# A third load buffer, a cast held in program order and a separate gate buffer in a two-model kernel

## The chip, the cores and the metric

The kernel runs on one core of a Trainium2 chip. The metric is the device time of one execution in microseconds. Three runs of the kernel before gave 2311.27 us (median), 2310.58 and 2315.97 us.

## The reference

The input is 512 tokens of width 1024, all in float32. Two hybrid layers come first, then one block of another kind. Cut to what matters here, a hybrid layer is:

```
h   = rmsnorm(x, pre_mix_g);  proj = h @ w_in          # 12 kinds of columns, gates among them
y_a = deltanet(proj) @ w_up_dn                         # its output is normed and gated by silu(z)
y_b = sliding_window_attention(proj) @ w_up_sw
mix = (sigmoid(gate_a) * y_a + sigmoid(gate_b) * y_b) @ w_o
x   = x + rmsnorm(mix, post_mix_g)
ff  = square(relu(rmsnorm(x, pre_mlp_g) @ w_ff1)) @ w_ff2   # 1024 -> 4096 -> 1024
x   = x + rmsnorm(ff, post_mlp_g)
```

The second block (a state-space branch, a pooling branch, gates, an output product and a last norm) is not touched by the change.

## The kernel before

Activations stand transposed: 8 tiles of 128 features by 512 tokens. Each float32 operand is kept as a high part `h` (a cast to float32r) and a low part `lo` (source minus `h`), and each product is three matmuls: `h·h`, `h·lo`, `lo·h`, in that order (`mm3`). A weight block is 1024x128. `load_w` (L225) fetches it by a DMA on the SyncE queue (SP) into a `raw` tile, of which there are two, casts it on ScalarE (ACT) to `h` (L241) and forms `lo` on VectorE (L242). The result goes to `wh`/`wl` rings of three, or, for weights that are kept for a second use, into tiles `kw` that a callback `keep` allocates. After `third(pool)` (L164), and once two more loads have gone by, every load whose running number leaves 2 when divided by 3 goes to an extra buffer `rawx` in that pool. In the kernel before this is on in the mixing stage, the last down stage and the second block.

Stages of a layer, as far as the change goes:

- **Mixing** (L1304). `fetch` (L1313) loads a tile from DRAM into a ring `fe` of three buffers. For each of 8 output blocks it fetches the deltanet output (`ogf`) and gate 0, multiplies them on VectorE (L1335), splits the product into `ah`, and after the attention branch's matmuls multiplies by gate 2 (L1340), which also stands in the `fe` ring. Then come 8 blocks with `w_up_dn` on `ah`, then 8 with `w_o`, the last in two halves of 256 tokens.
- **First six blocks of the MLP** (L1403 on). Six `w_ff1` blocks are run over the first half of the tokens, then again over the second, so the last three are kept. The residual and norm of the mixing stage's second half (`residual`, a generator that `tick` moves on after blocks 0 and 1) run beside them; its results are stored to DRAM (`xd_mid`) through a ring of four tiles `rt`.
- **Last down stage** (L1464 to L1508). The hidden tiles of the last quarter come from four pairs of blocks (`fast_pair`), the last of which feeds hidden tiles 6 and 7. `halves3` runs the first three `w_ff2` blocks over the first half of the tokens with tiles 7 and 6 last. Blocks 3 to 7 load their weight in the loop and keep it. After each block VectorE adds the result into `acc` (L1490) and `fs.add` squares it on ACT (L365). The second half runs the same eight blocks with the weights kept. `tick` there moves on the residual of the first half: its sums follow block 0, its broadcast block 1, the next norm's sums block 5, its broadcast block 6.

The order on each engine is not the order of the program: a planner simulates the kernel and, on each engine, issues what is ready, earlier traced instructions first. `tc.keep_in_program_order(i)` takes this freedom from one instruction: it is issued behind the instruction that was traced just before it on the same engine. `tick` uses it for TensorE: the first matmul after a tick is held behind what the tick issued, and what the tick issues first is held behind the block ahead of it.

Of the kernel before, what the change touches and what calls it, by code (L numbers as in the profile page):

```python
# [19 lines left out]
P = 128  # L20
# [3 lines left out]
KD = D // P  # L24
# [30 lines left out]
def body(  # L55
# [10 lines left out]
    V, S, G, DMA = nc.vector, nc.scalar, nc.gpsimd, nc.sync  # L66
# [89 lines left out]
    def t2(name, shape=(P, SEQ), dtype=F32):  # L156
        return tp.tile(list(shape), dtype, tag="t2", name=name, bufs=NT2)
# [6 lines left out]
    def third(pool):  # L164
        turn[1:] = pool, turn[0] + SKIP
# [56 lines left out]
            V.tensor_tensor(out=lo, in0=t, in1=f32(h), op=ALU.subtract)  # L222
            return h, lo

    def load_w(src, kn=KD, n=P, pool_h=False, keep=None):  # L225
        turn[0] += 1
        if turn[0] % 3 == 2 and turn[1] is not None and turn[0] > turn[2]:
            raw = turn[1].tile([P, kn, n], F32, tag="rawx", name="rawx", bufs=1)
        else:
            raw = wp.tile([P, kn, n], F32, tag="raw", name="raw", bufs=2)  # L230
        DMA.dma_start(out=raw, in_=src.rearrange("(k p) n -> p k n", p=P))
        h = lo = None
        if keep is not None:
            h, lo = keep(kn, n), keep(kn, n)
        if h is None:
            h = wp.tile([P, kn, n], F32R, tag="wh", name="wh", bufs=3)
            lo = wp.tile([P, kn, n], F32R, tag="wl", name="wl", bufs=3)
        if pool_h:
            G.tensor_scalar(out=h, in0=raw, scalar1=1.0, scalar2=0.0, op0=ALU.mult, op1=ALU.add)  # L239
        else:  # L240
            S.copy(out=h, in_=raw)  # L241
        V.tensor_tensor(out=lo, in0=raw, in1=f32(h), op=ALU.subtract)  # L242
        return h, lo

# [197 lines left out]
    def ticks(gen, at):  # L442
        cnt = [0]

        def tick():
            if cnt[0] in at:
                T.turn = True
                next(gen, None)
                T.turn = True
            cnt[0] += 1  # L450
        return tick
# [740 lines left out]
    def layer(l, st, nxt):  # L1192
# [4 lines left out]
        dg = [dp.tile([P, KD, SEQ], F32, name=f"dg{l}{i}") for i in range(3)]  # L1197
# [41 lines left out]
        for _ in range(5):  # L1239
            t = qa.tile([P, 2, 4, 256], F32R, tag="q8", name="kq", bufs=5)  # L1240
# [63 lines left out]
        with sbuf(f"mx{l}") as mp:  # L1304
            third(mp)
            def m2(name, dtype=F32R):
                t = mp.tile([P, 2, SEQ], dtype, tag="m2", name=name, bufs=NM2)
                return t[:, 0, :], t[:, 1, :]

            def keep(kn, n):  # L1310
                return mp.tile([P, kn, n], F32R, tag="m2", name="kw", bufs=NM2)

            def fetch(src, n, name):  # L1313
                t = mp.tile([P, SEQ], F32, tag="fe", name=name, bufs=3)
                DMA.dma_start(out=t, in_=src[:, n, :])
                return t

            def gate(i, n):
                t = fetch(dg[i], n, "gate")
                if (i, n) in plain:  # L1320
                    S.activation(out=t, in_=t, func=gate_fn[i])
                return t

            bo, ao = [], []
            for n in range(KD):
                hl = m2("bh")
                split(*hl, fetch(db, n, "bf"), eng=G)
                bo.append(hl)
            tb = []
            for n in range(KD):  # L1330
                if n % 2 == 0:
                    pair = m2("tb", F32)
                w = load_w(w_up_sw[l][:, n * P:(n + 1) * P])
                t = fetch(og, n, "ogf")
                V.scalar_tensor_tensor(out=t, in0=t, scalar=pcol("dn_norm", l), in1=gate(0, n), op0=ALU.mult, op1=ALU.mult)  # L1335
                hl = m2("ah")
                split(*hl, t)
                ao.append(hl)
                ps = dense(w, bo)
                V.tensor_tensor(out=pair[n % 2], in0=ps, in1=gate(2, n), op=ALU.mult)  # L1340
                tb.append(pair[n % 2])
            mix = []
            for n in range(KD):
                ps = dense(load_w(w_up_dn[l][:, n * P:(n + 1) * P]), ao)
                ta_ = gate(1, n)
                V.tensor_tensor(out=ta_, in0=ps, in1=ta_, op=ALU.mult)
                V.tensor_tensor(out=ta_, in0=ta_, in1=tb[n], op=ALU.add)
                hl = m2("mh")
                split(*hl, ta_)
                mix.append(hl)  # L1350
            mo = [mt.tile([P, SEQ], F32, tag="mo", name="mo", bufs=KD) for _ in range(KD)]
            mid = Stream("pre_mlp", l * KD, f"xd_mid{l}", mt, False)
            wk, tick = {}, None
            for i in range(2):
                ms = Stats(mt)
                for n in range(KD):
                    if i == 0:
                        wk[n] = load_w(w_o[l][:, n * P:(n + 1) * P], keep=keep if n >= 3 else None)
                    ps = dense_half(wk[n], mix, i)
                    V.tensor_copy(out=mo[n][:, HALVES[i]], in_=ps)  # L1360
                    ms.add(mo[n][:, HALVES[i]])
                    if i:
                        tick()
                pending = residual(st, mo, ms.rstd, "post_mix", l * KD, mid, i)
                if i == 0:
                    before = pending
                    tick = ticks(before, AT_O)
            finish(before)

        with sbuf(f"ff{l}") as ff, ExitStack() as es2:  # L1370
# [14 lines left out]
            def up(n, m=1):  # L1385
                return w_ff1[l][:, n * P:(n + m) * P], m == 2

            def down(g, n):
                return w_ff2[l][g * D:(g + 1) * D, n * P:(n + 1) * P], False
# [8 lines left out]
            with sbuf(f"kf{l}") as kp:  # L1398
                def keep(kn, n):
                    return kp.tile([P, kn, n], F32R, tag="kw", name="kw", bufs=2 * (NFF - 3))  # L1400

                tick = ticks(pending, AT_FF)
                wk = [load_w(up(n)[0], keep=keep if n >= 3 else None) for n in range(NFF)]  # L1403
                for i in range(2):
                    for n in range(NFF):
                        if i == 0:
                            hid.append(hidden())
                        relu2(dense_half(wk[n], mid.xs, i), hid[n][0][:, HALVES[i]], hid[n][1][:, HALVES[i]])
                        tick()
                        if i and n < 3:  # L1410
                            w.free("ring")
                    finish(pending)
                    w.fetch(1)
                tail.close()
            tail = ExitStack()
            tl = tail.enter_context(sbuf(f"tl{l}", "right"))
# [46 lines left out]
            kp = es2.enter_context(sbuf(f"kp{l}"))  # L1463
# [15 lines left out]
            wk = {}  # L1479
            for i in range(2):  # L1480
                fs = Stats(tr)
                for n in range(KD):
                    if i == 0 and n == 0:
                        wk = {j: w.take() for j in range(3)}
                        head = halves3([wk[j] for j in range(3)], i)
                    elif i == 0 and n >= 3:
                        wk[n] = load_w(down(3, n)[0], keep=keep)
                    ps = head[n] if i == 0 and n < 3 else dense_half(wk[n], hid, i)
                    ac = acc[n][:, HALVES[i]]
                    V.tensor_tensor(out=ac, in0=ps, in1=ac, op=ALU.add)  # L1490
                    fs.add(ac)
                    if i:
                        tick()

                def ff_rstd(i=i, fs=fs):
                    fm = small((P, 2), "fm")
                    V.scalar_tensor_tensor(out=fm, in0=fs.sums(), scalar=1.0 / D, in1=rs4[i], op0=ALU.mult, op1=ALU.mult)
                    V.tensor_scalar(out=fm, in0=fm, scalar1=EPS, scalar2=None, op0=ALU.add)
                    fr = power(fm, 2)
                    V.tensor_tensor(out=fr, in0=fr, in1=rs2[i], op=ALU.mult)  # L1500
                    return fr

                pending = residual(mid, acc, ff_rstd, "post_mlp", l * KD, xst, i)
                if i == 0:
                    before = pending
                    tick = ticks(before, AT_D)
# [17 lines left out]
    dg = dp.tile([P, 32, SEQ], F32, name="dg2")  # L1524
# [16 lines left out]
    with sbuf("kp2") as kp:  # L1541
        def keep(kn, n):
            return kp.tile([P, kn, n], F32R, tag="kw", name="kw", bufs=2 * NB2 - 6)
# [15 lines left out]
    with sbuf("ss") as sp:  # L1559
# [59 lines left out]
        for g8 in range(4):  # L1619
# [14 lines left out]
            for par in range(2):  # L1634
                V.tensor_copy(out=yv[:, par, 4 * g8:4 * g8 + 4],
                              in_=ps[64 * par:64 * par + 64].rearrange("p q (j c) -> p q j c", c=16))
# [52 lines left out]
    for c in range(4):  # L1689
        ps = dense(load_w(ssm_w_glu_2[0][:, c * P:(c + 1) * P], 4), glu)  # L1690
        t = t2("glt")
# [23 lines left out]
    wk = {}  # L1715
# [53 lines left out]
```

## Time and profile before

| what | value |
|---|---|
| profiled execution, its own time | 2315.69 us |
| its span, first to last instruction | 2313.9 us |
| mean granted TensorE clock | 0.982 |
| TensorE matmul busy / weight loads busy | 2243.0 us (97%) / 1954.5 us (84%) |
| VectorE, ScalarE, GpSimd busy | 1485.3, 952.1, 609.4 us |
| moved by DMA | 284.33 MB, mean 123 GB/s |

The span is the time from the first to the last instruction of the profiled execution; 1.8 us of its own time lie around it. Busy times of different engines overlap. A granted clock of 1 is 2.4 GHz, 0.5 is 1.2 GHz.

### The profile page before, as it was taken

To read this page: it belongs to the slowest core of one execution; us is meant where nothing else is said; L and a number is where in the kernel's file an instruction comes from. 1 tells how busy PE (TensorE), PEld (TensorE's weight loads), DVE (VectorE), ACT (ScalarE), POOL (GpSimd) and SP (SyncE) were. 2 spreads that over 40 slices of the span, in tenths; PEclk is the share of its full clock that TensorE was granted. 3 is DMA by queue.
4 is the path that set the end of the run, shared out by engine and by line. 5 is a ranking of instruction groups with operands and counts; after the bars stand their busy time and mean duration, and the time that the engine had idled before them with its cause. 6 is when DMAs were issued, how large, how long until landed. Compare 5 with 4: busy or idle time off the path is not lost. (4 is left out here: it accounts for less than half of the span.)

```text
span 2313.9 us, 37654 instructions
## 1 busy us (share of the span) xinstructions
PE 2243.0 (97%) x14460; PEld 1954.5 (84%) x14460; DVE 1485.3 (64%) x2958; ACT 952.1 (41%) x1726; POOL 609.4 (26%) x675
## 2 busy tenths in 40 slices
PE   8999999999999999999999999999999999899998
PEld 7867888887989899988678888889898898877788
DVE  5579793445576777665797934465777775435645
ACT  4554333333464354444533333334643444423333
POOL 1643420200336123246333202003351242200001
PEclk9999999999999999999999999999999999999999
DMA  5223424565453433342233345654434334563344
GB/s 177 62 72 87 101 83 128 172 200 160 121 157 92 128 107 98 116 125 58 77 87 88 92 127 182 201 164 126 136 101 118 114 97 123 169 165 117 108 131 146
DMA packets 466431, 284.33 MB, mean 123 GB/s; under 512 B 48502, under 2 KB 440012, under 8 KB 465740
## 3 DMA queue, kind: packets, MB, share of 16 engines
q1 hardware_dynamic: 462544, 280.69, 41.9%
q8 instruction: 114, 1.87, 0.3%
q10 hardware_dynamic: 3708, 1.24, 0.3%
q14 instruction: 65, 0.53, 0.1%
HBM read 235.76 MB, written 46.11 MB: 122 GB/s over the span
## 5 line engine op out<-in xcount | busy, mean ns | idle before, releaser
L78 PE MATMUL psm<-xsh,wh 128*128 128x512 f32 (+1 forms) x1136 | 445.6, 393 | 2.6 <-ACT wh L241 1.6
L78 PE MATMUL psm<-xsl,wh 128*128 128x512 f32 (+1 forms) x1136 | 432.6, 381 | 8.2 <-DVE xsl L342 4.2
L78 PE MATMUL psm<-xsh,wl 128*128 128x512 f32 (+1 forms) x1136 | 431.6, 380 | 0.0
L242 DVE TENSOR_TENSOR wl<-raw,wh 128x1024 fp32r<-128x1024 f32 (+2 forms) x179 | 213.3, 1192 | 89.9 <-ACT wh L241 63.6
L78 PEld LDWEIGHTS psm<-xsh,wh 128*128 128x128 f32 x1136 | 217.6, 192 | 48.4 <-issue 8.6
L78 PEld LDWEIGHTS psm<-xsl,wh 128*128 128x128 f32 x1136 | 218.1, 192 | 45.9 <-DVE xsl L342 5.5
L78 PEld LDWEIGHTS psm<-xsh,wl 128*128 128x128 f32 x1136 | 217.3, 191 | 40.9
L241 ACT CAST wh<-raw 128x1024 fp32r<-128x1024 f32 (+3 forms) x126 | 123.4, 980 | 253.6 <-PE psm L78 218.2
L370 POOL TENSOR_TENSOR sa<-sa,sq 128x256 f32<-128x256 f32 x54 | 51.5, 955 | 665.8 <-ACT sq L365 381.5
L78 PE MATMUL psm<-hh,wh 128*128 128x512 f32 (+1 forms) x480 | 177.1, 375 | 6.4 <-ACT hh L336 6.4
L78 PE MATMUL psm<-hl,wh 128*128 128x512 f32 (+1 forms) x480 | 177.7, 372 | 0.8 <-DVE hl L339 0.8
L78 PE MATMUL psm<-hh,wl 128*128 128x512 f32 (+1 forms) x480 | 176.7, 370 | 0.0
L221 ACT CAST wh<-raw 128x1024 fp32r<-128x1024 f32 x67 | 70.2, 1050 | 127.4 <-PE psm L78 76.2
L221 ACT CAST wh<-raws 128x1024 fp32r<-128x1024 f32 x63 | 66.0, 1047 | 127.9 <-PE psm L78 93.7
L222 DVE TENSOR_TENSOR wl<-raw,wh 128x1024 fp32r<-128x1024 f32 x67 | 97.4, 1454 | 26.0 <-ACT wh L221 23.5
L78 PEld LDWEIGHTS psm<-hh,wh 128*128 128x128 f32 x480 | 90.5, 191 | 22.8 <-ACT hh L336 7.0
L78 PEld LDWEIGHTS psm<-hl,wh 128*128 128x128 f32 x480 | 91.5, 191 | 16.4 <-DVE hl L339 1.3
L78 PEld LDWEIGHTS psm<-hh,wl 128*128 128x128 f32 x480 | 91.6, 191 | 15.1
L222 DVE TENSOR_TENSOR wl<-raws,wh 128x1024 fp32r<-128x1024 f32 x63 | 93.6, 1486 | 13.2 <-ACT wh L221 13.2
L239 POOL TENSOR_SCALAR wh<-raw 128x1024 fp32r<-128x1024 f32 (+1 forms) x53 | 62.9, 1186 | 121.0 <-PE psm L78 104.0
L78 PE MATMUL psm<-ah,wh 128*128 128x512 f32 x256 | 83.0, 405 | 5.2 <-ACT ah L336 5.0
L78 PE MATMUL psa<-xsh,wh 128*128 128x256 f32 x288 | 82.3, 286 | 0.0
(670 smaller groups left out, 5662.5 us busy)
## 6 DMA issues: line engine op xcount, KB each, us to landing
raw<-in_w_in_dram SPq DMA_DIRECT2D x130, 512.0 KB, 3.9
raw<-in_w_ff_dram SPq DMA_DIRECT2D x75, 512.0 KB, 4.1
raws<-in_w_ff_dram SPq DMA_DIRECT2D x51, 512.0 KB, 4.3
gate<-dg SPq DMA_DIRECT2D x48, 256.0 KB, 4.4
rawx<-in_w_in_dram SPq DMA_DIRECT2D x14, 512.0 KB, 4.1
raw<-in_w_up_sw_dram SPq DMA_DIRECT2D x12, 512.0 KB, 5.0
raw<-in_w_up_dn_dram SPq DMA_DIRECT2D x11, 512.0 KB, 4.5
raw<-in_w_o_dram SPq DMA_DIRECT2D x10, 512.0 KB, 4.7
```

What stands on the lines that cost most here:

```text
L78: return s.issue(nc.tensor.matmul(*a, **k))
L221: S.copy(out=h, in_=t)
L222: V.tensor_tensor(out=lo, in0=t, in1=f32(h), op=ALU.subtract)
L239: G.tensor_scalar(out=h, in0=raw, scalar1=1.0, scalar2=0.0, op0=ALU.mult, op1=ALU.add)
L241: S.copy(out=h, in_=raw)
L242: V.tensor_tensor(out=lo, in0=raw, in1=f32(h), op=ALU.subtract)
L370: (G if s.n in POOL_ACC else V).tensor_tensor(out=s.acc, in0=s.acc, in1=sq, op=ALU.add)
```

## The change

`load_w` gets a parameter `pin`, which holds the ACT cast in program order; the loads of blocks 3 to 7 in the last down stage set it. `third(kp)` turns the third raw buffer on for the first six blocks of the MLP and `third(None)` turns it off behind them. Gate 2 of the mixing stage is fetched into a tile of the ring `t2` (four buffers of the same size, used there by nothing else in this stage).

```
-    def load_w(src, kn=KD, n=P, pool_h=False, keep=None):
+    def load_w(src, kn=KD, n=P, pool_h=False, keep=None, pin=False):
...
-            S.copy(out=h, in_=raw)
+            i = S.copy(out=h, in_=raw)
+            if pin:
+                tc.keep_in_program_order(i)
         V.tensor_tensor(out=lo, in0=raw, in1=f32(h), op=ALU.subtract)
...
             def gate(i, n):
-                t = fetch(dg[i], n, "gate")
+                if i == 2:
+                    t = t2("gate2")
+                    DMA.dma_start(out=t, in_=dg[i][:, n, :])
+                else:
+                    t = fetch(dg[i], n, "gate")
...
                 tick = ticks(pending, AT_FF)
+                third(kp)
                 wk = [load_w(up(n)[0], keep=keep if n >= 3 else None) for n in range(NFF)]
...
                     w.fetch(1)
+                third(None)
                 tail.close()
...
                     elif i == 0 and n >= 3:
-                        wk[n] = load_w(down(3, n)[0], keep=keep)
+                        wk[n] = load_w(down(3, n)[0], keep=keep, pin=True)
```

## Rows read from the trace of the kernel before

**Rows 1.** The page, busy time of each engine (share of the span, instructions).
```profile
PE 2243.0 (97%) x14460; PEld 1954.5 (84%) x14460; DVE 1485.3 (64%) x2958; ACT 952.1 (41%) x1726; POOL 609.4 (26%) x675
```
**Rows 2.** Waits of TensorE: us in total, times, longest us.
```profile
PE psm L78 <- ACT hh L336: 6.4, 2, 4.4
...
PE psm L78 <- ACT ft L1380: 5.4, 2, 2.7
PE psm L78 <- ACT ah L336: 5.0, 2, 2.8
```
**Rows 3.** Timeline of ACT, second layer's last pair and after: start, us, instruction.
```profile
1919.52 1.04 ACT L241 CAST kw<-raw 128x1024 fp32r<-128x1024 f32 x1 [1.64 <-DMA raw<-in_w_ff_dram]
...
1930.63 0.42 ACT L365 ACTIVATE sq<-acc 128x256 f32<-128x256 f32 x1 [1.05 <-DVE acc L1490]
```
**Rows 4.** Timeline of TensorE in the same stretch.
```profile
1923.79 1.01 PE L78 MATMUL psm<-hh,wh 128*128 128x256 f32 x3 [4.42 <-ACT hh L336]
```
**Rows 5.** Timeline of ACT, first layer's last pair.
```profile
943.95 1.04 ACT L241 CAST kw<-raw 128x1024 fp32r<-128x1024 f32 x1 [1.26 <-DMA raw<-in_w_ff_dram]
```
**Rows 6.** Stretches: us, each engine's busy us (instructions), granted clock, DMA share, GB/s.
```profile
530.00:536.00 6.00, 6.00 (x16) 4.70 (x16) 4.82 (x6) 1.85 (x3) 0.00 (x0) 0.52 0.70 220
943.00:953.00 10.00, 7.22 (x36) 6.72 (x37) 4.77 (x8) 4.32 (x7) 0.73 (x1) 0.66 0.56 162
1508.00:1511.00 3.00, 2.78 (x8) 2.23 (x8) 2.31 (x4) 1.45 (x2) 0.00 (x0) 0.58 0.89 285
1919.00:1929.00 10.00, 5.00 (x23) 4.30 (x22) 5.42 (x7) 6.97 (x10) 0.00 (x0) 0.66 0.61 174
1929.00:1944.00 15.00, 15.00 (x126) 15.00 (x127) 5.42 (x12) 2.67 (x7) 1.94 (x2) 1.00 0.13 36
```
**Rows 7.** Timeline of VectorE, mixing stage of the first layer.
```profile
514.53 0.75 DVE L1335 SCALAR_TENSOR_TENSOR ogf<-ogf,prm,gate 128x512 f32<-128x512 f32 x1 [4.09 <-DMA gate<-dg]
...
516.93 0.69 DVE L1340 TENSOR_TENSOR tb<-psm,gate 128x512 f32<-128x512 f32 x1
...
522.03 0.75 DVE L1335 SCALAR_TENSOR_TENSOR ogf<-ogf,prm,gate 128x512 f32<-128x512 f32 x1 [3.28 <-DMA gate<-dg]
```
**Rows 8.** Timeline of the SP queue there.
```profile
517.05 1.12 SPq L1315 DMA_DIRECT2D gate<-dg  x2
```
**Rows 9.** Timeline of the SP queue, first six blocks of the second layer's MLP.
```profile
1598.53 0.39 SPq L231 DMA_DIRECT2D raw<-in_w_ff_dram  x1
1598.97 5.09 SPq L1072 DMA_DIRECT2D lbr<-in_ssm_b_re_dram  x1
...
1612.79 0.41 SPq L401 DMA_DIRECT2D xd_mid<-rt  x1
```
**Rows 10.** Timeline of ACT there.
```profile
1610.18 1.04 ACT L241 CAST kw<-raw 128x1024 fp32r<-128x1024 f32 x1 [10.37 <-DMA raw<-in_w_ff_dram]
```
**Rows 11.** Timeline of VectorE there.
```profile
1611.25 1.23 DVE L242 TENSOR_TENSOR kw<-raw,kw 128x1024 fp32r<-128x1024 f32 x1 [7.58 <-ACT kw L241]
```
**Rows 12.** Timelines of VectorE, then ACT, behind one block of the last down stage.
```profile
1934.91 0.42 DVE L1490 TENSOR_TENSOR acc<-psm,acc 128x256 f32<-128x256 f32 x1 [1.48 <-PE psm L78]
...
1935.43 0.42 ACT L365 ACTIVATE sq<-acc 128x256 f32<-128x256 f32 x1 [2.46 <-DVE acc L1490]
```
**Rows 13.** Instructions of tile kw: count, then ns min/median/max, first and last start.
```profile
L241 ACT CAST kw<-raw x24: 1030/1044/1055, 573.5 to 1993.4; 128x1024 fp32r<-128x1024 f32 x24
L242 DVE TENSOR_TENSOR kw<-raw,kw x24: 1215/1225/1762, 574.6 to 1994.5; 128x1024 fp32r<-128x1024 f32 x24
```
**Rows 14.** Timeline of TensorE, second half of the same stage: sums and broadcasts of the residual.
```profile
1946.23 0.50 PE L78 MATMUL psa<-ones,sa 128*128 128x1 f32 x4
...
1965.03 0.60 PE L78 MATMUL psa<-ident,rstd 128*128 128x128 f32 x4
```
**Rows 15.** Chain of waits in order of time, second block (start, us, what).
```profile
2058.00 7.09 PE psm L78 x23
2065.09 1.14 PE psa L81 x16
```

## The prediction

> **What bounds the kernel now.** I read the page first: TensorE is busy for 2243.0 of 2313.9 us [rows 1], so all its gaps together are 70.9 us, and an edit can win only what it takes out of gaps or what it gives the clock back. Then the waits of TensorE [rows 2]: three of its waits, two times each (once in each layer), lie where the change works. `hh` (last pair) costs 4.4 and 2.0 us, `ft` (first six blocks) 2.7 and 2.7, `ah` (mixing) 2.8 and 2.2. Then the timelines around them, to see who is late, and last the stretches behind them [rows 6]: after such a gap the granted clock is near 0.5, the 1.2 GHz level. In 1919 to 1929 us 23 matmuls took 5.00 us, 0.217 each; in the next 15 us 126 took 15.00, 0.119 each. That slow stretch counts as busy, and belongs to the price of a gap.
>
> **Part 1, the third gate.** In the mixing stage VectorE's product of `ogf` and gate 0 waits 4.09 and 3.28 us for a gate's landing, and the products follow each other at 522.03 - 514.53 = 7.5 us [rows 7]. The two gate loads are issued at 517.05 [rows 8], just behind the gate-2 product that starts at 516.93 and frees their buffer [rows 7]. One block of 24 matmuls over 512 tokens takes some 5.7 us (24 times twice 0.119), so `ah` falls behind its users until TensorE stands. With gate 2 in a ring of its own, gate 0 of the next block can be issued when the product before it ends, 514.53 + 0.75 = 515.3, 1.7 us sooner: 7.5 - 1.7 = 5.8 us, about TensorE's own pace, and TensorE starts on `ah` only eight blocks later. I let both gaps go: 2.8 + 2.2 = 5.0. The low clock behind them goes too: (1 - 0.52) x 6.00 = 2.9 in the first layer, (1 - 0.58) x 2.78 = 1.2 in the second [rows 6]. Together **-9.1**. Bounds: 0 (the pace stays) to -9.1. The DMAs are the same in number and size, and the four `t2` tiles have no other user in the stage. Late next are the weight casts, which leave no gap of this size.
>
> **Part 2, the third raw buffer in the first six blocks.** By the count of loads it takes the third and the sixth of the six in layer 0, but only the fifth in layer 1. The trouble is the sixth load: in layer 1 SP issued it at 1598.53, when a buffer came free, between the table loads of the second block, one of which kept SP busy for 5.09 us [rows 9]. Its cast began at 1610.18, after ACT had stood for 10.37 us [rows 10], and VectorE for 7.58 [rows 11]; `ft`, queued behind the cast on ACT, was the 2.7 us wait of TensorE. With a third buffer the sixth load is issued ahead of the tables (in layer 1 it takes the buffer that the fifth had), so both waits of 2.7 go: 5.4. What comes late next is the residual of the second half, which the cast also held up: its first store left SP only at 1612.79, behind the tables [rows 9], and the four `rt` tiles are freed by these stores. The third buffer doesn't move that. I take half of the gaps, which may turn into a wait for the residual, and about half of a slow stretch like 2.3 us per layer: **-5**. Bounds: -10.6 (all of 5.4, and 5.2 of slow clock like the two stretches below) to +2: the new pool lies where tiles of the mixing stage lay, so its first load must wait for one of those to be read for the last time, SP standing in front of the residual's stores meanwhile.
>
> On this a page of the Trainium skill bears, "DMA: Bandwidth & Descriptors", section "Queues, rings and completion order": on each DMA engine the descriptors of one issuing queue are taken in ring order. By that rule everything that stands behind the table loads keeps its place whatever the raw buffers do, and part 2 would be worth nothing; the trace shows 11.65 us from issue to cast for the load that stood among them, which agrees, and no row of before shows the stores without the tables.
>
> **Part 3, the pinned casts.** What it takes away: in the last pair ACT had the cast of a kept weight queued ahead of the pair's squares and casts. In layer 1 it waited 1.64 us for its DMA and ran 1.04 [rows 3]; in layer 0 1.26 and 1.04 [rows 5]. That made the gaps of 4.4 and 2.0; the one of 4.42 stands in [rows 4]. Pinned, the cast is behind the pair. The pair's own five ACT steps remain in front of TensorE, so I give 3.5 of 4.4 and 1.5 of 2.0. The slow clock behind: 36 matmuls in 7.22 us against 36 x 0.119 = 4.3 is 2.9, and 23 in 5.00 against 2.7 is 2.3 [rows 6]. Together **-10.2** (-5 to -11.6).
>
> What it adds: the pin holds a cast behind the ACT instruction traced just before it. For block 3 that is not a cast of the pair but the square of block 2, for block 4 the square of block 3, up to block 7. Before, all five casts ran ahead of the squares: the third square began at 1930.63 [rows 3], when TensorE was already on kept weights without a gap, 126 matmuls in 15.00 us [rows 6]. Now a ring closes: block n's matmuls need its cast, the cast stands behind the square of n-1, this needs the sum into `acc`, and that the matmuls of n-1. The price of one turn: from the start of the sum, 1934.91, to the end of the square, 1935.43 + 0.42, is 0.94 [rows 12]; the cast is 1.04; then two matmuls can run, and the third of each three needs `lo`, which takes 1.22 on VectorE [rows 13], so 1.22 - 2 x 0.119 = 0.98 more. That is 0.94 + 1.04 + 0.98 = 3.0 us, for five blocks in two layers **+30**. The clock: ten blocks with gaps of 2.0 and 1.0 between them; at the low level one takes 24 x (0.217 - 0.119) = 2.4 more. Bounds 0 and 24; I take a third, **+8**, since the gaps of before that were followed by a slow stretch were 2 us or longer, and each such stretch ended while TensorE ran on.
>
> Can the gaps be filled? The planner does issue later traced matmuls into a gap: in the second block projections written behind the transposes run before them [rows 15]. Here block 0 of the second half is free, and blocks 3 to 5 once their weights are cast; 1, 2, 6 and 7 are held behind the ticks. But the residual of the first half starts only when block 7's square is done, and it runs from the sums at 1946.23 to the broadcast at 1965.03 [rows 14], with the next stage right behind. If the second half's blocks are spent early, TensorE stands there instead. It saves at most one block a layer, 24 x 0.119 = 2.9, as the sums needn't wait for block 0: the floor of the added wait is 30 - 5.8 = 24. The held casts keep raw buffers longer too, but the loads of the next stage then still have the second half, 8 x 2.9 = 23 us, to land. VectorE and GpSimd have nothing behind these waits that is due before the residual.
>
> **The sum.** -9.1 - 5 - 10.2 + 30 + 8 = +13.7. The profiled execution took 2315.69 us (1.8 around its span): 2329.4. It lies 4.4 above the median of 2311.27; the forecast for the median is 2311.27 + 13.7 = **2325.0**.
>
> **Rivals.**
> - *The residual waits behind the tables.* Part 2 gives 0 instead of -5: 2330. For it: the first store at 1612.79 [rows 9]. Against: the sixth load's place in the queue is freed. The ring order of the page above is this case.
> - *The clock stays low through the pinned blocks.* +24 instead of +8: 2341. For it: a gap of 2.0 was followed by a stretch at 0.66 [rows 6]. Against: within such stretches it came back by itself.
> - *The gaps are filled and the residual follows anyway (faster).* One mechanism: four second-half blocks, 11.4 us, go into 15 us of gaps in each layer, and the first half's residual, no longer mixed with their sums and squares on VectorE, ACT and GpSimd, shrinks by as much as it starts later. Left are 3.6 us a layer, 7.2, and no slow clock: 7.2 - 24.3 = -17, 2294. It decides if the residual's 18.8 us shrink to the 11.5 that the four blocks left behind it cover. Against: each of its eight pieces passes through VectorE, GpSimd and ACT in turn whatever else they do.
> - *The pin costs nothing* (the casts come behind the pair and still ahead of the squares, the change not doing what the code says): -24.3, 2287.
>
> **How the numbers follow.** Chances: forecast 0.52, tables 0.12, low clock 0.14, filled 0.10, no cost 0.12. The forecast's own range is 2305 to 2345: at the low end the floor of 24 without slow clock against the full gains, 24 - 9.1 - 5 - 10.2 - 5.6 (part 2 at its best) = -6; at the high end 30 + 16 of slow clock - 12 of gains = +34. A measurement of this kernel can tell about 0.3%, 7 us, from no change. Faster by more: the case without cost, 0.12, and 0.08 of the filled one, 0.20. Within 7 us: 0.02 of the filled one, 0.02 of the tables and 0.14 of the forecast, its low end, 0.18. Slower: the other 0.62. The range of 2297 to 2347 leaves out the case without cost and a top of some 0.06.
>
> **What would show it.** Right: in the last down stage squares and `kw` casts alternate on ACT, TensorE waits for `ACT kw` and `DVE kw` five times in each layer, or else stands some 12 us before the next stage; no `ah` wait in the mixing stage; the sixth `w_ff1` load issued ahead of the tables. Wrong: five casts still ahead of the squares, or TensorE without a gap from the last pair to the next stage.

## The result, and the profile after

The changed kernel takes 2345.86 us (median), the kernel before beside it 2313.62: ratio 1.0138, 95% interval 1.0117 to 1.0160, so +32 us (27 to 37). The forecast was +13.7, 2325.0. The direction came as forecast and the time lies just below the top of the range (2347), but the loss is more than twice the forecast one. The profiled execution has a span of 2346.6 us, 32.7 more than before.

First the page: TensorE's busy time (beside [rows 1]) rose by 10.7 us with the same 14460 instructions, and PEclk, the granted clock in 40 slices, shows a 7 in two places where all were 9.

```profile
PE 2253.7 (96%) x14460; PEld 1965.7 (84%) x14460; DVE 1489.4 (63%) x2958; ACT 945.7 (40%) x1722; POOL 607.4 (26%) x675
...
PEclk9999999999999999799999999999999997999999
```

TensorE's waits after (us in total, times, longest). Of [rows 2], `hh` and `ah` are gone; `ft` has grown from 5.4 to 10.1; `kw`, on ACT and on VectorE, is new, and POOL's `sa` (the sums) rose from 7.3 to 13.8. (One more wait for `kw`, the first of layer 0, 2.09 us, stands under VectorE's `sa` in this list.)

```profile
PE psm L78 <- ACT kw L241: 17.8, 9, 2.1
PE psa L78 <- POOL sa L372: 13.8, 10, 3.3
PE psm L78 <- ACT ft L1386: 10.1, 2, 6.1
...
PE psm L78 <- DVE kw L244: 5.5, 8, 0.8
```

The ring stands as the prediction drew it. ACT in layer 0's last down stage (start, us, instruction; idle before it and who ended that): a square, a cast, then 6 to 7 us of nothing.

```profile
945.58 0.42 ACT L367 ACTIVATE sq<-acc 128x256 f32<-128x256 f32 x1 [6.00 <-DVE acc L1498]
945.91 1.03 ACT L241 CAST kw<-raw 128x1024 fp32r<-128x1024 f32 x1
953.87 0.42 ACT L367 ACTIVATE sq<-acc 128x256 f32<-128x256 f32 x1 [6.93 <-DVE acc L1498]
954.19 1.03 ACT L241 CAST kw<-rawx 128x1024 fp32r<-128x1024 f32 x1
```

TensorE there: two waits a turn, 1.96 and 0.76.

```profile
955.27 0.39 PE L78 MATMUL psm<-hh,kw 128*128 128x256 f32 x1 [1.96 <-ACT kw L241]
955.49 0.28 PE L78 MATMUL psm<-hl,kw 128*128 128x256 f32 x1
956.53 0.51 PE L78 MATMUL psm<-hh,kw 128*128 128x256 f32 x2 [0.76 <-DVE kw L244]
```

And the stretches, one for each pinned block (columns as in [rows 6]). Here lies most of the miss: 24 matmuls keep TensorE busy for 4.65 to 5.72 us where 24 x 0.119 is 2.9, at granted clocks of 0.57 to 0.78. (The last stretch holds the fifth pinned block and one block of the second half.)

```profile
939.60:947.00 7.40, 4.65 (x25) 4.24 (x25) 2.11 (x4) 1.35 (x2) 0.00 (x0) 0.77 0.26 73
947.00:955.00 8.00, 5.72 (x24) 5.13 (x24) 1.62 (x2) 1.13 (x2) 0.64 (x1) 0.57 0.22 66
955.00:962.80 7.80, 4.90 (x24) 4.40 (x24) 2.08 (x3) 1.54 (x3) 0.09 (x1) 0.78 0.00 0
962.80:970.40 7.60, 4.90 (x24) 4.49 (x24) 2.08 (x3) 1.34 (x3) 0.00 (x0) 0.78 0.20 55
970.40:978.00 7.60, 7.49 (x48) 7.29 (x48) 1.44 (x2) 0.14 (x2) 0.00 (x0) 0.78 0.21 57
```

Above 0.119 a matmul that is 27.66 - 145 x 0.119 = 10.4 us in this layer, some 21 in both; not all of it is the clock, as a run below shows. The two profiled executions, lined up at the same instructions, differ by -8.9 us in the mixing stages, -1.6 in the first six blocks, -7.9 at the last pairs, +49.8 in the pinned stretches, and by +1.3 in all the rest together.

In the first six blocks SP's queue (start, us, load) shows the sixth load of layer 0, the `rawx` at 625.88, still among the tables:

```profile
611.80 0.34 SPq L1061 DMA_DIRECT2D row<-in_ssm_lam_re_dram  x1
612.20 1.37 SPq L1069 DMA_DIRECT2D dt<-in_ssm_log_dt_dram  x2
613.62 0.63 SPq L1074 DMA_DIRECT2D lbr<-in_ssm_b_re_dram  x1
615.34 0.40 SPq L189 DMA_DIRECT2D raw<-in_w_ff_dram  x1
615.79 5.73 SPq L1074 DMA_DIRECT2D lbr<-in_ssm_b_re_dram  x1
621.63 2.59 SPq L189 DMA_DIRECT2D raw<-in_w_ff_dram  x1
624.26 1.53 SPq L1074 DMA_DIRECT2D lbi<-in_ssm_b_im_dram  x1
625.88 1.85 SPq L231 DMA_DIRECT2D rawx<-in_w_ff_dram  x1
```

### The profile page after: what moved, and what is told of

It reads as the page before. It is cut to its first block, busy times and chain, and to the rows that moved or that the text cites. A ratio compares the mean times of both kernels' runs of the same rounds, so it can differ in the third digit from the quotient of the medians.

```text
span 2346.6 us, 37655 instructions
## 1 busy us (share of the span) xinstructions
PE 2253.7 (96%) x14460; PEld 1965.7 (84%) x14460; DVE 1489.4 (63%) x2958; ACT 945.7 (40%) x1722; POOL 607.4 (26%) x675
## 5 line engine op out<-in xcount | busy, mean ns | idle before, releaser
L241 ACT CAST wh<-raw 128x1024 fp32r<-128x1024 f32 (+2 forms) x125 | 122.3, 980 | 280.0 <-PE psm L78 246.4
L78 PE MATMUL psm<-hh,kw 128*128 128x256 f32 x320 | 75.8, 330 | 25.4 <-ACT kw L241 17.8
L78 PEld LDWEIGHTS psm<-hh,kw 128*128 128x128 f32 x320 | 61.9, 233 | 29.6 <-ACT kw L241 22.2
```

The source lines that it names most:

```text
L78: return s.issue(nc.tensor.matmul(*a, **k))
L241: i = S.copy(out=h, in_=raw)
```

## Experiments

Times are medians of each group of runs, against the kernel before on the same chip; a difference from it goes by the ratio. Diffs are against the kernel before unless said otherwise.

**The three parts.** Part 3 alone:

```diff
-                        wk[n] = load_w(down(3, n)[0], keep=keep)
+                        wk[n] = load_w(down(3, n)[0], keep=keep, pin=True)
```

> The kernel before with part 3 alone (the pinned casts). Theory A (the ring and the clock were both under-priced in the forecast; read from the two profiles): the pinned blocks cost 51 us in both layers, the last pair gives 8 back, so +43, 2356 us; TensorE waits 12.6 us a layer for ACT kw and DVE kw, and one pinned block of 24 matmuls takes about 5.0 us where one at full clock takes 2.9. Theory B (the forecast's own terms, and something else in the changed kernel costs the rest): -10.2 + 30 + 8 = +28, 2341 us. Theory C (most of the cost comes from the three parts together, the third raw buffer delaying the next loads): under +20.

2356.43 against 2311.66, ratio 1.0188 (1.0173 to 1.0204), +43.5 us: theory A. `ACT kw` 19.9 us in 10 waits, `DVE kw` 5.5 in 8.

Parts 1 and 2, against the changed kernel:

```diff
-                        wk[n] = load_w(down(3, n)[0], keep=keep, pin=True)
+                        wk[n] = load_w(down(3, n)[0], keep=keep)
```

> The changed kernel without the pin: parts 1 and 2. Theory A (sizes read from the two profiles): the mixing stage gives 8.9 and the first six blocks 1.6, so -10.5, 2303 us, with one gap of some 6 us left in layer 0's first six blocks (the sixth load issued behind the tables) and one of some 4 us in layer 1's (the residual's stores behind the tables). Theory B (the forecast's sizes): -14, 2299 us, no gap over 2 us there. The waits at the last pair (4.4 and 2.0 us) are back in both.

2302.19, ratio 0.9952 (0.9936 to 0.9969), -11.1: theory A, though B's -14 lies within the interval; the gaps decide, 5.90 us in layer 0 and 4.30 in layer 1, both at `ft`.

Part 1 alone:

```diff
-                t = fetch(dg[i], n, "gate")
+                if i == 2:
+                    t = t2("gate2")
+                    DMA.dma_start(out=t, in_=dg[i][:, n, :])
+                else:
+                    t = fetch(dg[i], n, "gate")
```

> The kernel before with part 1 alone (gate 2 in tiles of its own). Theory A: no wait of TensorE for ah in the mixing stage and the products of VectorE less than 6 us apart, -9, 2304.5 us; the first six blocks keep their two gaps of 2.7 us. Theory B (the shift of the mixing stage came from something else in the changed kernel): the ah waits of 2.8 and 2.2 us stay and the time is within 3 us of before.

2305.48, ratio 0.9968 (0.9956 to 0.9980), -7.4 (-4.6 to -10.2): theory A in the time and in TensorE's waits, `ah` being gone. The products less than 6 us apart that it also expected did not come: in layer 0 the eight start from 470.29 to 520.21 us, 7.1 each on average, and in the kernel before from 471.16 to 527.84, 8.1 each. With the run before, part 2 is worth -11.1 + 7.4 = -3.7, give or take 3. The sum of the three, -7.4 - 3.7 + 43.5 = +32.4, is the measured whole.

**Casts behind the pair, not behind the squares.** The five loads and casts are written in one go, ahead of the first sum and square:

```diff
                         head = halves3([wk[j] for j in range(3)], i)
-                    elif i == 0 and n >= 3:
-                        wk[n] = load_w(down(3, n)[0], keep=keep)
+                        wk.update((j, load_w(down(3, j)[0], keep=keep, pin=True)) for j in range(3, KD))
```

> The kernel before with the five kept weights loaded and cast in one go, written ahead of the first sum and square and each pinned behind the one before it, so that the first stands behind the last pair's casts and none behind a square. Theory A (the price of part 3 is the ring through sum, square and cast, and only that): the last pair's gap shrinks as in the changed kernel, no wait for ACT kw or DVE kw over 0.5 us a layer, -8, 2305.5 us. Theory B (a cast behind the pair comes too late whatever stands between): waits for ACT kw of some 2 us a layer and a slow stretch behind them, 0 or worse.

2296.57, ratio 0.9933 (0.9917 to 0.9948), -15.5: theory A in the waits, with a gain above its -8. No wait for `kw` is left, only one of 0.78 at `acc` in each layer. The stretches from the last pair to the next stage give -5.1 and -6.5 us, -11.6 together. The other 4 lie in stretches that the edit doesn't touch; in the profile this run is 5 us ahead of the kernel before already when layer 0's last pair begins. ACT casts right behind the pair and squares between:

```profile
936.77 0.62 ACT L338 CAST hh<-fq 128x512 fp32r<-128x512 f32 x1
937.30 1.99 ACT L241 CAST kw<-raw 128x1024 fp32r<-128x1024 f32 x2
939.19 1.04 ACT L241 CAST kw<-rawx 128x1024 fp32r<-128x1024 f32 x1
940.14 0.41 ACT L367 ACTIVATE sa<-acc 128x256 f32<-128x256 f32 x1
940.46 0.71 ACT L367 ACTIVATE sq<-acc 128x256 f32<-128x256 f32 x2
```

**Idle or clock.** The ring as in part 3 alone, with its gaps filled by spare matmuls (16 go ahead of each pinned block, and by the same means six more ahead of its first product with `lo`; the edit is cut to the first of the two):

```diff
+                    fill = None
+                    if i == 0 and n >= 3:
+                        def fill(cnt, dm=ps_ax((P, HS))):
+                            T.turn = True
+                            for q in range(cnt):
+                                T.matmul(dm, lhsT=wk[0][0][:, q % KD, :], rhs=hid[q % KD][0][:, HALVES[0]], start=q == 0, stop=q == cnt - 1)
+                            T.turn = True
+                        fill(16)
```

> Part 3 alone as in the change (each cast behind the square of the block before), with spare matmuls of 256 tokens into an unused PSUM tile in TensorE's gaps: 16 ahead of each pinned block, 6 ahead of its first product with lo. The ring through sum, square and cast is the same; only TensorE's idleness is taken away. Theory A (about 20 us of the pinned blocks' price is the low clock that follows the gaps): 24 matmuls take 2.9 us again, -8 + 2 x (5 x 3.0 + 2.5) = +27, 2338 us, 18 below the run with part 3 alone. Theory B (the blocks are slow for another reason): 2356 us or more.

2334.29, ratio 1.0109 (1.0086 to 1.0133), +25.2: theory A, 18.3 us below part 3 alone, each against the kernel before on its own chip. Stretches of part 3 alone (layer 0, layer 1), then with the gaps filled:

```profile
942.00:980.00 38.00, 27.53 (x141) 25.91 (x142) 8.47 (x12) 5.40 (x8) 0.72 (x1) 0.69 0.18 50
1944.70:1983.00 38.30, 27.72 (x143) 26.11 (x142) 8.58 (x12) 5.40 (x8) 0.73 (x1) 0.69 0.19 55
```

```profile
943.00:980.00 37.00, 34.13 (x261) 32.30 (x261) 11.12 (x18) 6.95 (x11) 2.69 (x3) 0.98 0.21 59
1929.00:1966.00 37.00, 33.66 (x257) 31.83 (x258) 11.63 (x19) 7.15 (x12) 2.89 (x3) 0.98 0.25 72
```

The same ring, over a hundred matmuls more in as long a stretch, and the clock at 0.98, near its 2.4 GHz level, instead of 0.69. On ACT the squares of the ring follow each other every 6.13 us, where part 3 alone has 7.53 to 8.28. From the last pair to the next stage the two layers are 7.5 and 7.7 us shorter than with idle gaps, 15.2 together; the rest of the 18 lies in stretches where these runs differ by a few us among themselves. So some 15 us are the clock. The count above 0.119 a matmul gives 21 for part 3 alone too, but with the gaps filled it still gives 34.13 - 261 x 0.119 = 3.1 and 33.66 - 257 x 0.119 = 3.1: so some 6 of the 21 are not the clock. That they go with each stop and start of TensorE is argued, not shown.

**One turn instead of five:**

```diff
-                        wk[n] = load_w(down(3, n)[0], keep=keep)
+                        wk[n] = load_w(down(3, n)[0], keep=keep, pin=n == 3)
```

> Part 3 with the pin on the first of the five casts only, so that all five stand behind one square: one turn of the ring in each layer. Theory A (the price goes by the turn, idle 2.7 us and some 2 us of low clock each): -11.6 + 2 x 4.7 = -2, 2309 us. Theory B (the first gap alone brings the low clock down on all the blocks behind it): +8 or more, 2319.

2304.49, ratio 0.9975 (0.9964 to 0.9986), -5.8, better than theory A's -2 and far from B. In the stretches from the last pair to the next stage, against the casts behind the pair, one turn costs 3.4 and 3.2 us a layer, five cost 26.7 and 27.4, of which the wait for the sums is 2.5 and 2.9: 4.9 a turn. (The times of the two runs differ by 9.7, 3 more than these stretches.) Of one turn 2.5 and 3.3 us are waits for `kw`, though the clock fell behind it too, to 0.76 from 946 to 951 us. Of five, 12.6 us a layer are waits for `kw`, 2.5 a turn; the rest is mostly the clock.

**Part 2.** Next, part 1 and the mended pin together, the base for what follows:

> Part 1 as in the change, and part 3 as it should have been (five kept weights cast behind the last pair and ahead of the squares); no third raw buffer. If the parts add up: the two runs alone gave -6.2 and -15.1 us, their stretches of the trace -9.9 and -11.6, so -21.4, 2290 us. Rival: the two share a cause (a lower clock over the whole run), then the sum falls short, 2294 or more.

2290.37 (ratio 0.9909, interval 0.9894 to 0.9924), -21.0, where the two runs alone give -22.9: they add up within the interval. On this base, part 2 with two extra buffers:

```diff
-            raw = turn[1].tile([P, kn, n], F32, tag="rawx", name="rawx", bufs=1)
+            raw = turn[1].tile([P, kn, n], F32, tag="rawx", name="rawx", bufs=nbx[0])
...
+                third(kp)
+                nbx[0] = 2
```

> The run with part 1 and the mended pin, with part 2 added, and its third raw buffer doubled for these six loads. Theory A (two things failed part 2: in layer 0 the sixth load needs the one extra buffer that the third load still holds; in both layers the residual's stores wait behind the table loads): the sixth load is issued ahead of the tables in both layers, and a wait of TensorE of about 4 us is left in both, now at the residual; no gain over the same kernel without part 2 by more than 2 us, 2288 to 2292. Theory B (the extra buffer alone failed): the waits of 2.5 and 2.7 us and the slow clock behind them go, 7 us less, 2283.

2288.43, ratio 0.9900 (0.9884 to 0.9917): 1.9 us, theory A in the time. A wait of 4.16 us at `ft` is left in layer 1; layer 0 keeps three of 1.2 to 1.4 for `xsl` instead of the 4 us that theory A had there. On the same base, late tables and no third buffer:

```diff
-                DMA.dma_start(out=dst[64 * half:64 * half + 64],
-                              in_=src[0, grs].rearrange("(i two) p c -> two p i c", two=2)[half])
+                with tc.issue_after(after.ins):
+                    DMA.dma_start(out=dst[64 * half:64 * half + 64],
+                                  in_=src[0, grs].rearrange("(i two) p c -> two p i c", two=2)[half])
```

(`after` is the residual's last store; the `crow` loads likewise.)

> The run with part 1 and the mended pin, without a third raw buffer, but with the eight loads of the tables' large inputs (lbr, lbi, crow) queued on SP behind the last store of the second half's residual. Theory A (the table loads in SP's queue bound the first six blocks): the sixth load lands some 6 us sooner, the first residual store leaves some 5 us sooner, and of the stretch's gaps (6.1 us in layer 0, 6.6 in layer 1) and the slow clock behind them most go: -8 to -14, 2276 to 2282 us. Theory B (ACT's order or the four rt tiles bound it, wherever the tables stand): within 3 us of the same kernel with the tables early, 2290. Theory C (the tables then stand before the loads of the next stage): a wait at the token sums or the second group, slower.

2292.59, ratio 0.9920 (0.9905 to 0.9935): my theory A fell; the time is theory B's. With `lbr` and `lbi` out of the way ACT still waited 10.0 us for the sixth load. Both edits at once:

> Both at once: tables late and the third raw buffer, doubled. Theory A (with the tables out of the way the raw buffer is worth nothing): within 2 us of the run with late tables alone. Theory B (each alone only uncovers the other): 4 us or more below it, 2274 or less.

2280.13, ratio 0.9868 (0.9854 to 0.9883): 10 us under the base and 12.5 under the run with late tables: theory B, though not down to its 2274. So something still stood in front of the sixth load in the run with late tables. Its stretches show what: from 614 to 624 us the DMA engines moved next to nothing, 0 to 7 GB/s. The same in the base, behind the two `dt` loads (issued 608.96 and 609.72):

```profile
608.00:612.00 4.00, 4.00 (x36) 4.00 (x35) 3.00 (x7) 3.26 (x7) 1.24 (x4) 1.00 0.05 10
612.00:616.00 4.00, 3.37 (x29) 3.17 (x28) 2.39 (x4) 1.73 (x4) 1.89 (x2) 1.00 0.05 0
616.00:620.00 4.00, 4.00 (x36) 4.00 (x36) 0.48 (x1) 0.00 (x0) 0.74 (x1) 1.00 0.13 16
620.00:624.00 4.00, 2.89 (x25) 2.68 (x23) 0.00 (x0) 0.00 (x0) 0.00 (x0) 1.00 1.04 199
```

ACT in the base: the cast of the sixth load, issued at 612.51, waits for its data.

```profile
624.26 1.04 ACT L241 CAST kw<-raw 128x1024 fp32r<-128x1024 f32 x1 [10.47 <-DMA raw<-in_w_ff_dram]
```

Two runs moved the `dt` loads behind the residual's last store, one with the other tables late, one with them in place:

```diff
-            DMA.dma_start(out=dt[64 * half:64 * half + 64, :],
-                          in_=ssm_log_dt_2[0, grs].rearrange("(i two) -> two i", two=2)[half].partition_broadcast(64))
+            with tc.issue_after(after.ins):
+                DMA.dma_start(out=dt[64 * half:64 * half + 64, :],
+                              in_=ssm_log_dt_2[0, grs].rearrange("(i two) -> two i", two=2)[half].partition_broadcast(64))
```

> The run with part 1, the mended pin and late tables, without a third raw buffer, with the two dt loads (64 x 8 single elements each) also queued behind the last residual store. Theory A (these two loads keep the DMA queue from moving anything for some 8 us, the share of the DMA engines being 0.03 to 0.08 at 0 to 7 GB/s from 614 to 624 us of the run with late tables): the sixth load lands in some 5 us, the gap at ft goes, and the time is that of the run with both edits, 2280 us, with no third buffer. Theory B (the buffer is needed): 2290 to 2293 us.

> Part 1 and the mended pin, no third raw buffer, the lbr, lbi and crow loads where they were, and only the two dt loads late. Theory A (the dt loads are all of it): within 3 us of the run above, 2280 us. Theory B (the lbr and lbi loads, which kept SP for 5 us, hold up the sixth load and the stores too): 2286 us or more.

2292.36 and 2296.33: both theories A missed the time, and had the mechanism. The cast of the sixth load began 4.0 and 4.7 us after its issue, and the gaps in the first six blocks went, but for one of 0.99. But `dt` then stood in front of the token sums' loads. ACT, of the first of the two:

```profile
651.49 0.72 ACT L322 ACTIVATE tsb<-tsb,prm 128x512 f32<-128x512 f32 x1 [10.85 <-DMA tsb<-xd_mid]
```

TensorE waited 7.0 us in one layer and 7.6 in the other for that, and 9.1 in each layer of the second run. The stop had only moved. So it was taken away instead, by loading `dt` as rows of 16 values (the `Exp` then picks even and odd columns):

```diff
-        for half in range(2):
-            DMA.dma_start(out=dt[64 * half:64 * half + 64, :],
-                          in_=ssm_log_dt_2[0, grs].rearrange("(i two) -> two i", two=2)[half].partition_broadcast(64))
+        dt16 = tl("dt16", (P, NG, 2))
+        DMA.dma_start(out=dt16.rearrange("p i two -> p (i two)"), in_=ssm_log_dt_2[0, grs].partition_broadcast(P))
```

> Part 1 and the mended pin, no third raw buffer, the tables' loads in their places, but dt loaded as one row of 16 values to all 128 partitions instead of 2 x 64 x 8 single elements, its even and odd columns picked by the two halves of the Exp. Theory A (the two dt loads stop the DMA queue for some 8 us, and whatever stands behind them waits, the sixth raw load here, the token sums' loads where dt was moved): no stretch of 0 GB/s behind it, the sixth load lands within 5 us of its issue, no gap over 1.5 us in the first six blocks nor at the seventh to tenth, 2274 to 2280 us, 10 to 16 under the same kernel with the old dt loads (2290). Theory B (the queue is stopped by the number of small packets of lbr and lbi too): the sixth load takes 8 us or more, 2285 or more.

2275.31, ratio 0.9839 (0.9823 to 0.9856), -37.2, some 16 under the base, each against the kernel before on its own chip: theory A. TensorE has no gap left at `ft` over 0.4 us. The stretches and the cast now:

```profile
612.00:616.00 4.00, 4.00 (x35) 4.00 (x35) 2.95 (x7) 2.85 (x8) 1.41 (x3) 1.00 0.30 79
616.00:620.00 4.00, 3.37 (x29) 3.16 (x28) 2.81 (x4) 2.15 (x5) 2.15 (x2) 1.00 0.57 129
620.00:624.00 4.00, 4.00 (x36) 4.00 (x35) 2.40 (x5) 2.70 (x6) 1.79 (x3) 1.00 0.95 229
```

```profile
621.24 1.05 ACT L241 CAST kw<-raw 128x1024 fp32r<-128x1024 f32 x1 [3.02 <-DMA raw<-in_w_ff_dram]
```

All four `lbr` and `lbi` loads are still ahead of the residual's stores here, and took 2.6 us of SP in all; the 5 to 8 us that SP stood on one of them belonged to `dt`. And the same with part 2 as the change has it:

> The same with part 2 as the change has it (one third raw buffer in the first six blocks). Theory A (the third buffer was worth what it moved ahead of the dt loads, and nothing without them): within 3 us of the run above. Theory B (the buffer count is a bound of its own): 4 us or more below it.

2276.15, ratio 0.9834 (0.9819 to 0.9850): theory A, the third buffer is worth nothing once `dt` is a row. The run without it is the best version: 2275 us, 37 under the kernel before.

## Why the prediction was wrong

The step that failed is the clock term of part 3, "I take a third, **+8**". It measured some 15 us: that much came back when the gaps were filled. The reason given, that slow stretches "ended while TensorE ran on", came from single gaps, and for a single turn it nearly holds (3.3 us, close to the 3.0 of the ring). It says nothing of gaps that return every 7 to 8 us: [rows 6] had no such stretch. The clock is 7 of the 18 us that the forecast fell short, the largest single term. The profiles put the others at 3.4 (part 2 gave less), 2.3 (so did the last pairs) and some 5 for the ring without its clock (49.8 - 15.2 = 34.6, where +30 stood).

The bound of 24 held, and the rival at that bound, 2341 us at 0.14, was nearest to the 2345.9 measured. In part that is luck: its clock of 24 was too high by 9, and the other terms too low by about as much.

The Trainium skill's page "TensorE: Matmul & The Clock Gate", section "A second HAM failure mode: psum-queue depth-cycling", tells of a kernel whose frequent short idles between groups of matmuls made the clock swing between its levels. The trace agrees (0.57 to 0.78 with gaps of 1.96 and 0.76), and the forecast did not weigh it.

Term by term, forecast and measured:
- Part 1, -9.1: right in size, -8.9 in the trace and -7.4 (-4.6 to -10.2) alone, and right that the `ah` gaps would go. The pace was not the 5.8 us a block forecast but 7.1 in layer 0; that was enough. Runs without part 1 differ in the mixing stage by up to 2.5 us a layer, so the time alone carries the size.
- Part 2, -5: the gain was over-sized, -1.6 in the trace, -3.7 give or take 3 in the times. Two sentences of the step were wrong. That "the sixth load is issued ahead of the tables" holds in layer 1 (the last of the six is issued at 1607.43, ahead of `row`), not in layer 0, where the one extra buffer held the third load until 618.19 and SP then stood among the tables. And the half that I let turn into a wait for the residual became nearly all: 3.96 us at `ft` in layer 1. The rival of the residual behind the tables was right in its effect and wrong in its culprit: not `lbr`, whose 5.09 us on SP I read as its own [rows 9], but the `dt` loads ahead of it, as the runs with `dt` moved or as rows show.
- Part 3, what it takes away, -10.2: about right; -7.9 in the changed kernel, -11.6 by the casts behind the pair, where no ring follows.
- Part 3, the ring, +30: right in its waits. Part 3 alone shows 19.9 + 5.5 us of waits for `kw` and 2.5 + 2.9 for the sums, 30.8; the 6 us beside the waits and the clock were not in the sum. That the casts stood behind squares, and not behind the pair, was read from the code and is seen on ACT.
- The gaps were not filled: the blocks of the second half stayed behind, but for one a layer (it fills the fifth turn's wait for `lo`, so VectorE's `kw` stands four times a layer), and the wait for the sums grew by what that saved.

## To carry to other kernels

A pin behind "the previous instruction" holds an instruction behind whatever was traced last, so write it where that is what should be waited for: moving five loads ahead of the loop turned +43 us into -15. Price repeated short gaps on TensorE with more of the low clock than follows one gap: 4.9 us a turn here against 3.3. Where a load takes long to land (11.7 us here from issue to cast), look at the DMA engines' share and GB/s before counting buffers: if nothing moves, look for a load of single elements in front.

## What the hardware showed

Two loads of 64 x 8 single elements (2 KB each) kept the SP queue's transfers at 0 GB/s for some 8 us, at a share of 0.05 of the 16 DMA engines (16 x 0.05 = 0.8, about one engine's worth), while loads of 512 KB stood behind them. Loaded as 128 rows of 16 values, `dt` landed 2.5 us after its issue and nothing stopped.

That the pieces are many and short is not enough. By their shapes the four `lbr` and `lbi` loads are 512 runs of 16 elements each, twice as many runs as the two `dt` loads have. First the packets of the base from 610 to 618 us, behind `dt`, then those of the run with `dt` as rows from 614 to 618 us, with `lbr` and `lbi`: 99 a us against 434.

```profile
DMA packets 793, 0.00 MB, mean 0 GB/s; under 512 B 793, under 2 KB 793, under 8 KB 793
```

```profile
DMA packets 1737, 0.11 MB, mean 27 GB/s; under 512 B 1731, under 2 KB 1737, under 8 KB 1737
```

The Trainium skill's page "DMA: Bandwidth & Descriptors", section "Rules for kernel authors", says that a strided last dimension becomes one descriptor for each element and should be made contiguous. The trace agrees as far as it goes: 793 packets in 8 us carried under 5 KB, and the two loads have 1024 elements. The runs add that the cost falls on every load queued behind.

Whether the queue's rings or the making of its descriptors stood still, no run here tells, nor whether it is the length of the runs or that 64 partitions read the same few elements. Nor does a run tell from how many turns of the ring on each costs more than a single one.
